# A hybrid attention and recurrence layer on one core: a fourth chunk of x turned by VectorE and DRAM, and the first stage written out by hand

## The chip, the cores and the metric

The kernel runs on one core of a Trainium2 chip. The metric is device time in microseconds (us); three runs of the kernel before gave a median of 626.83 us (626.64 to 627.36). Lower is better.

## The reference, cut to what matters

One layer takes x (512 tokens by 2048 features, float32), normalises it, projects it to 4608 columns, runs eight heads of attention and a gated linear recurrence on the parts, gates both, and projects back. The first step is the one that matters here:

```python
def rms_norm(x, w):
    xf = x.astype(jnp.float32)
    y = xf * lax.rsqrt(jnp.mean(xf * xf, axis=-1, keepdims=True) + EPS)
    return (y * w.astype(jnp.float32)).astype(x.dtype)

h = rms_norm(x, norm_w)
proj = jnp.einsum('bsd,de->bse', h, w_in)
q, k, v, g_attn, xr, g_lru = jnp.split(proj, SPLITS, axis=-1)
lru_out = lru_group(xr, ...)
mixed = jnp.concatenate([rms_norm(attn_out, attn_norm_w) * jax.nn.silu(g_attn),
                         rms_norm(lru_out, lru_norm_w) * jax.nn.silu(g_lru)], axis=-1)
return x + jnp.einsum('bse,ed->bsd', mixed, w_out)
```

## The kernel before

Every float32 operand of a product is split into a high part (rounded to float32r) and a low part (the rest), and each product is three TensorE passes: high by high, high by low, low by high (`mm3`, lines 152 to 155). ScalarE writes most high parts, VectorE the low parts.

The first stage is the projection to the first half of `xr` (`proj_feat(C_XR, a1, ...)`, lines 379 to 406 and 1212 to 1232). It needs x with features on the partitions, so that each of x's sixteen 128-feature columns has to be turned. x comes in eight chunks of 256 features (512 KB each, `xload`, tile `b`), and the matching rows of `w_in` in eight pieces of 512 KB (`wraw`, tile `wr`, a ring of three). A chunk c is 24 matmuls of 128x512: four output blocks, two columns, three passes. The mean square of x is not needed for this: its factor `rbc` multiplies the result at the end, so the squares (`xsquare`) can be late.

A chunk is turned in one of two ways. Chunks 0 to 4 (`TURNED = 5`): eight 128x128 transposes on TensorE against the identity (`xturn`, line 253), then ScalarE takes the high part out of PSUM (line 258) and VectorE the low one (line 261). Chunks 5 to 7: VectorE transposes 32x32 blocks within 32 partitions (`blocks`, line 281, tile `xu`), SyncE writes the result to DRAM (`put_aside`, line 289, `xd<-xu`, one transfer of 512 KB), and four transfers of 128 KB bring it back with the blocks on the right partitions (`bring_back`, line 296, `xu<-xd`, each to 32 partitions). Then ScalarE scales it in place (line 338) and rounds it (line 339), and VectorE subtracts (line 339). In this text, for a chunk n: Ln is its load, Wn the load of its weights, Bn its block transposes, Dn the write to DRAM, Rn the four reads back, Vn the scaling and splitting, Sn the splitting of Wn on ScalarE (line 218) and VectorE (line 219), Qn its four squares.

TensorE and SyncE run in written order through this stage. ScalarE and VectorE do so only up to step (1, 2) (`s2.close()`, line 1224); after that a scheduler orders them by priority and by `issue_after` links. What is issued when is set by a table of steps, `moves` (line 1195): a generator per chunk (`xchunk`) is advanced one phase at each mention. Each transfer on SyncE's queue waits until the eighth one before it has landed, as its eight completion semaphores go round.

The last projection to the output (`outputs`, lines 1008 to 1145) streams `w_out` in units; `feed2` (line 991) loads one unit's second row block, for the second half of the columns (g = 1) as one transfer of 512 KB (line 995).

Of the kernel before, what the change touches and what calls it, by code (L numbers as in the profile page):

```python
# [11 lines left out]
F32 = mybir.dt.float32  # L12
# [37 lines left out]


B = 32
TURNED = 5
NQ = P // B


# [7 lines left out]
def hybrid_kernel(  # L64
# [53 lines left out]
    def nm(s):  # L118
        cnt[0] += 1
        return f"{s}_{cnt[0]}"  # L120
# [108 lines left out]

    xh, xl = [None] * KT, [None] * KT  # L230
    ssq = const([P, NT, KT // 2], "ssq")
    highs, x_parts, squared = {}, [], []

    def xload(c, nk=1):

        xc = b4(shape=(P, NT, 2 * P))
        for k in range(nk):
            ks = slice(k * 2 * P // nk, (k + 1) * 2 * P // nk)
            cs = slice(c * 2 * P + ks.start, c * 2 * P + ks.stop)
            nc.sync.dma_start(xc[:, :, ks], xf[:, cs].rearrange("(t p) d -> p t d", p=P))  # L240
            yield xc

    def behind(those):
        stack = ExitStack()
        for ins in those:
            stack.enter_context(tc.issue_after(ins))
        return stack

    def xturn(xc, kk, then=None):
        pt = mm()  # L250
        for t in range(NT):
            ks = slice(kk % 2 * P, (kk % 2 + 1) * P)
            nc.tensor.transpose(pt[:, t * P : (t + 1) * P], xc[:, t, ks], ident)  # L253
        if then:
            then()
        xh[kk], xl[kk] = x2(), x2()
        with behind(split_done[-1] if kk > 3 else ()):
            highs[kk // 2] = nc.scalar.activation(
                xh[kk], pt, AF.Identity, scale=nw[:, kk : kk + 1]
            ).ins  # L260
        nc.vector.scalar_tensor_tensor(
            xl[kk], pt, nw[:, kk : kk + 1], f(xh[kk]), op0=ALU.mult, op1=ALU.subtract
        )

    def xsquare(xc, c):
        for t in range(NT):
            if c >= TURNED:
                nc.scalar.activation(
                    xc[:, t, :], xc[:, t, :], AF.Square, accum_out=ssq[:, t, c : c + 1]
                )  # L270
                continue
            square = nc.vector.scalar_tensor_tensor(
                xc[:, t, :], xc[:, t, :], 1.0, xc[:, t, :], op0=ALU.mult, op1=ALU.mult,
                accum_out=ssq[:, t, c : c + 1],
            )
            if c == 1:
                squared.append(square.ins)

    def blocks(u, t, src):

        nc.vector.transpose(
            u[:, :, :, t, :].rearrange("p b k r -> p k b r"),
            src.rearrange("p (k b c) -> p k b c", k=2, c=B),
        )
# [15 lines left out]
    def in_order(v):  # L300
        return v.rearrange("p (t i r) -> p i t r", t=NT, i=NQ)

    def xchunk(c):
        with tc.high_priority(AHEAD):
            (xc,) = xload(c)
        yield
        if c < TURNED:
            with tc.high_priority(AHEAD):
                for k in range(2):
                    xturn(xc, 2 * c + k)  # L310
            if c == 2:
                yield
            with behind(split_done[2][1:] if c == 2 else ()):
                xsquare(xc, c)
            yield
            return
        u, back = (
            ring.tile([P, NQ, 2, NT, B], F32, name=nm("xu")) for ring in (aring, hring)
        )
        with tc.high_priority(AHEAD), tc.issue_after(squared[-1] if c == TURNED else split_done[3][1]):  # L320
            for t in range(NT):
                blocks(u, t, xc[:, t, :])
        yield
        with tc.high_priority(AHEAD):
            there = put_aside(u, "xd", KT // 2 - TURNED)
        with tc.issue_after(highs[TURNED - 1]):
            xsquare(xc, c)
        yield
        with tc.high_priority(AHEAD):
            bring_back(back, there)  # L330
        yield
        with tc.high_priority(AHEAD), behind(split_done[-1]):
            for k in range(2):
                kk = 2 * c + k
                xh[kk], xl[kk] = x2(), x2()
                hi, lo = (in_order(v) for v in (xh[kk], xl[kk]))
                v = back[:, :, k]
                nc.scalar.activation(v, v, AF.Identity, scale=nw[:, kk : kk + 1])
                x_parts[:] = nc.scalar.copy(hi, v).ins, nc.vector.tensor_sub(lo, v, f(hi)).ins
        yield  # L340

    last_pool = [None]

# [8 lines left out]
    def rows(dst, col, dg):  # L352

        shape = [P, NT, P]
        part = [const([P, NT], nm("part")) for _ in range(2)]
        parts = [dg() for _ in part]
# [12 lines left out]
        yield  # L369
# [621 lines left out]
    def feed2(g, i, got):  # L991

        m = mixed[i][0] // (2 * P)
        x_ = in_wr()
        nc.sync.dma_start(x_.rearrange("p j e -> p (j e)"), block(m, 1, 2 * g, 2))
        if g == 0:
            z = in_av(1)
            nc.sync.dma_start(z[:, 0], t4[m])
        else:
            z = kept_t2.pop(i)  # L1000
            nc.vector.tensor_add(z, z, x_[:, 1:2])
        yield
        got.append(split(x_))
        yield
        got.append(split(z))
        yield
# [160 lines left out]
    with tc.high_priority():  # L1167
        xs, ws = xload(0, 2), wraw(w_in, 0, C_XR, 2)
        nc.scalar.dma_start(nw_st, norm_w.rearrange("(k p) -> k p", p=P))
        xc, raw = next(xs), next(ws)  # L1170
        next(xs), next(ws)
        table = const([P, 1], "table")
        nc.scalar.activation(table, ones[:, :1], AF.Exp)
        first = []

        def split_first():
            first.append(wsplit(raw, 0, nc.vector.tensor_copy))

        columns(nw, nw_st)
        xturn(xc, 0, split_first)  # L1180
        busy(WARM2)
    stats = xstats()
    chunks = [xchunk(c) for c in range(1, KT // 2)]

    raws = {}

    def fetch_x(c):
        with tc.high_priority(AHEAD):
            (raws[c],) = wraw(w_in, c * 2 * P, C_XR)

    def split_x(c):
        with tc.high_priority(AHEAD), behind(x_parts):
            given[c] = [wsplit(raws[c], k) for k in range(2)]

    moves = {
# [6 lines left out]
    }  # L1202

    def move(step):
        for name in moves.get(step, "").split():
            n = int(name[1])
            if name[0] == "x":
                next(chunks[n - 1])
            else:
                (fetch_x if name[0] == "w" else split_x)(n)  # L1210

    for step in proj_feat(C_XR, a1, first, given):
        if step is None:
            with tc.high_priority():
                first.append(wsplit(raw, 1, nc.vector.tensor_copy))
                xturn(xc, 1)
            xsquare(xc, 0)
            move(None)
            given[1] = wload(w_in, 2 * P, C_XR)
# [10 lines left out]
        if (c, e) in ((4, 3), (KT // 2 - 1, 0)):  # L1230
            with tc.high_priority(AHEAD), tc.issue_after(split_done[-1][1]):
                next(stats)

    s1.close()
    last_x = loads_done["lru"] = loads_done[nc.sync]
# [213 lines left out]
```

## Time and profile before

| | |
|---|---|
| median of three runs | 626.83 us |
| span of the profiled execution, first to last instruction | 625.3 us |
| median less that span | 1.5 us |
| TensorE busy | 620.3 us (99%) |
| VectorE busy | 494.8 us (79%) |
| ScalarE busy | 353.2 us (56%) |
| bytes moved by DMA | 127.61 MB |

The span is that of one execution under the profiler; the 1.5 us are what lies around it in the timed runs. TensorE's busy time is a union of modelled intervals: a matmul is shown as 0.39 us long while the next one starts 0.23 us after it, so the starts, not the durations, give its pace. For SyncE, a row of the timeline is the issue of a transfer, not the transfer.

### The profile page before, as it was taken

How to read it: one execution, taken by the hardware profiler on the slowest of the kernel's cores; microseconds unless marked ns; L12 is line 12 of the kernel's file. 1: busy time of each engine (PE TensorE's matmuls, PEld its weight loads, DVE VectorE, ACT ScalarE, POOL GpSimd, SP SyncE). 2: the span in 40 equal slices, each digit the busy share in tenths (PEclk: the TensorE clock that was granted, in tenths of full speed). 3: DMA queues.
4: the chain of work that ended last, by engine and by line, in shares of the span. 5: the costliest groups of instructions: out<-in, count | busy, mean ns of one | idle time of the engine just before them, and what ended most of it. 6: DMA issues, size and time to landing. Idle time of an engine off the chain costs nothing.

```text
span 625.3 us, 8281 instructions
## 1 busy us (share of the span) xinstructions
PE 620.3 (99%) x2758; PEld 512.8 (82%) x2758; DVE 494.8 (79%) x796; ACT 353.2 (56%) x617; POOL 101.7 (16%) x134
## 2 busy tenths in 40 slices
PE   9999999999999999999999999999999999999997
PEld 7888888888888888888888888888888888888886
DVE  5967979986699875987887888549979866886886
ACT  3764899479945823545485448428445633443441
POOL 0000210112003531622123223100310101010010
PEclk9999999999999999999999999999999999999999
DMA  8878785859774599479658646923995677896262
GB/s 289 293 210 253 179 206 163 175 136 197 236 231 140 169 235 250 103 204 273 186 175 258 201 140 192 265 79 106 261 248 185 210 253 240 293 327 233 68 202 101
DMA packets 73595, 127.61 MB, mean 204 GB/s; under 512 B 6617, under 2 KB 29265, under 8 KB 73553
## 3 DMA queue, kind: packets, MB, share of 16 engines
q1 hardware_dynamic: 65664, 109.65, 56.7%
q0 software_dynamic: 7712, 17.31, 14.3%
q8 instruction: 21, 0.34, 0.2%
q14 instruction: 22, 0.17, 0.1%
q10 hardware_dynamic: 176, 0.14, 0.1%
HBM read 110.29 MB, written 37.75 MB: 237 GB/s over the span
## 4 chain that ended last, share of the span: by engine, by line
PE 99%; DVE 0%; issue 0%; POOL 0%; POOLq 0%
PE pj L153 20%; PE pj L154 20%; PE pj L155 20%; PE mm L1029 14%; PE pj L1029 11%; PE mm L155 3%; PE mm L154 3%; PE mm L153 3%; PE pj L388 2%; PE mm L253 1%; PE mm L1156 1%; PE mm L829 0%; PE mm L367 0%; DVE cb L1058 0%; PE mm L189 0%
## 5 line engine op out<-in xcount | busy, mean ns | idle before, releaser
L153 PE MATMUL pj<-x,wh 128*128 128x512 f32 x368 | 143.5, 390 | 0.0
L155 PE MATMUL pj<-x,wl 128*128 128x512 f32 x368 | 143.2, 389 | 0.0
L154 PE MATMUL pj<-x,wh 128*128 128x512 f32 x368 | 143.2, 389 | 0.0
L218 ACT CAST wh<-wr 128x512 fp32r<-128x512 f32 x142 | 84.9, 620 | 78.9 <-PE pj L154 31.2
L219 DVE TENSOR_TENSOR wl<-wr,wh 128x512 fp32r<-128x512 f32 x144 | 99.9, 724 | 19.7 <-ACT wh L218 18.6
L881 ACT CAST wh<-wr 128x1024 fp32r<-128x1024 f32 (+1 forms) x72 | 60.8, 862 | 75.7 <-PE mm L1029 34.6
L882 DVE TENSOR_TENSOR wl<-wr,wh 128x1024 fp32r<-128x1024 f32 (+1 forms) x72 | 68.8, 985 | 30.5 <-ACT wh L881 30.3
L155 PEld LDWEIGHTS pj<-x,wl 128*128 128x128 f32 x368 | 69.1, 188 | 14.5
L153 PEld LDWEIGHTS pj<-x,wh 128*128 128x128 f32 x368 | 69.1, 188 | 14.3
L154 PEld LDWEIGHTS pj<-x,wh 128*128 128x128 f32 x368 | 69.1, 188 | 14.3
L153 PE MATMUL pj<-wh,x 128*128 128x512 f32 x192 | 74.7, 389 | 0.0
L155 PE MATMUL pj<-wh,x 128*128 128x512 f32 x192 | 74.7, 389 | 0.0
L154 PE MATMUL pj<-wl,x 128*128 128x512 f32 x192 | 74.7, 389 | 0.0
L905 POOL DMA_DIRECT2D t<-in_w_out_dram x40 | 33.5, 891 | 156.6 <-DMA t<-in_w_out_dram 99.4
L1029 PE MATMUL mm<-wh,ml 128*128 128x512 f32 x126 | 49.0, 389 | 0.0
L1029 PE MATMUL mm<-wh,mh 128*128 128x512 f32 x126 | 49.0, 389 | 0.0
L1029 PE MATMUL mm<-wl,mh 128*128 128x512 f32 x126 | 49.0, 389 | 0.0
L155 PEld LDWEIGHTS pj<-wh,x 128*128 128x128 f32 x192 | 36.0, 188 | 7.6
L153 PEld LDWEIGHTS pj<-wh,x 128*128 128x128 f32 x192 | 36.0, 188 | 7.5
L154 PEld LDWEIGHTS pj<-wl,x 128*128 128x128 f32 x192 | 36.0, 188 | 7.4
L706 POOL TENSOR_SCALAR p<-p,sm 128x512 f32<-128x512 f32 x32 | 24.3, 762 | 89.4 <-DVE sm L705 89.4
L1029 PE MATMUL pj<-wl,mh 128*128 128x512 f32 (+1 forms) x100 | 38.5, 385 | 0.0
(201 smaller groups left out, 1053.6 us busy)
## 6 DMA issues: line engine op xcount, KB each, us to landing
wr<-in_w_in_dram SPq DMA_DIRECT2D x71, 512.0 KB, 5.1
wr<-in_w_out_dram SPq DMA_DIRECT2D x24, 512.0 KB, 5.1
t<-in_w_out_dram POOLq DMA_DIRECT2D x40, 256.0 KB, 6.9
wr<-t SPq DMA_DIRECT2D x40, 256.0 KB, 5.4
pd<-u SPq DMA_DIRECT2D x16, 512.0 KB, 3.0
pt<-pd SPq DMA_DIRECT2D x64, 128.0 KB, 3.6
t<-in_w_out_dram SPq DMA_DIRECT2D x24, 256.0 KB, 5.4
t<-t SPq DMA_DIRECT2D x16, 256.0 KB, 5.1
```

The lines of the kernel that those rows point to most:

```text
L153: nc.tensor.matmul(acc, lh, rh, start=start, stop=False)
L154: nc.tensor.matmul(acc, lh, rl, start=False, stop=False)
L155: nc.tensor.matmul(acc, ll, rh, start=False, stop=stop)
L218: copy(hi, raw[:, k, :]).ins,
L219: nc.vector.tensor_sub(lo, raw[:, k, :], f(hi)).ins,
L253: nc.tensor.transpose(pt[:, t * P : (t + 1) * P], xc[:, t, ks], ident)
L388: nc.tensor.matmul(acc[e], w[:, e * P : (e + 1) * P], x_[2 * c + k], start=c == k == j == 0, stop=False,)
L706: last_pool[0] = nc.gpsimd.tensor_scalar(p, p, sm, 0.0, op0=ALU.mult, op1=ALU.add).ins
L881: nc.scalar.copy(hi[:, to], b)
L882: nc.vector.tensor_sub(lo[:, to], b, f(hi[:, to]))
L905: nc.gpsimd.dma_start(dst, src, accum_op=ALU.add)
L1029: nc.tensor.matmul(dst[s][:, es], lh[:, ts_], rh[:, es], start=i == ends_[0] and j == 0, stop=i == ends_[1] and j == 2,)
```

## The change

`TURNED` goes from 5 to 4: chunk 4 is no longer turned on TensorE but goes, as chunks 5 to 7 do, by VectorE and DRAM. The generator `xchunk` and its `issue_after` links are replaced by one short function per phase, and the table `moves` names every phase (L, W, T and H for turning, B, D, R, V, S, Q, and Z for the statistics). `s2.close()` moves from step (1, 2) to (5, 3), so that ScalarE and VectorE keep the written order until then. The squares come late: those of chunks 2 and 3 at step (2, 2), those of 6 and 7 at (3, 2). Apart from the first stage, `feed2` splits its load into two of 256 KB for g = 1 and the first six units.

```diff
-TURNED = 5
+TURNED = 4
...
+    def block_x(c):
+        units[c] = [ring.tile([P, NQ, 2, NT, B], F32, name=nm("xu")) for ring in (aring, hring)]
+        for t in range(NT):
+            blocks(units[c][0], t, chunk[c][:, t, :])
+
+    def aside_x(c):
+        units[c][0] = put_aside(units[c][0], "xd", KT // 2 - TURNED)
+
+    def back_x(c):
+        bring_back(units[c][1], units[c][0])
+
+    def whole_x(c):
+        for k in range(2):
+            v = units[c][1][:, :, k]
+            nc.scalar.activation(v, v, AF.Identity, scale=nw[:, 2 * c + k : 2 * c + k + 1])
+        for k in range(2):
...
+            nc.scalar.copy(hi, v)
+            nc.vector.tensor_sub(lo, v, f(hi))
...
-        x_ = in_wr()
-        nc.sync.dma_start(x_.rearrange("p j e -> p (j e)"), block(m, 1, 2 * g, 2))
+        if g and i < 6:
+            for j in range(2):
+                nc.sync.dma_start(x_[:, j], block(m, 1, 2 * g + j))
+        else:
+            nc.sync.dma_start(x_.rearrange("p j e -> p (j e)"), block(m, 1, 2 * g, 2))
...
-        (2, 0): "x5 x4 x5", (2, 1): "x4 w3", (2, 2): "x6 x7", (2, 3): "w4 s3",
+        (2, 0): "B6 D6 R5 W5 R6 Q5 Q5 V4",
...
-        if (c, e) == (1, 2):
+        if (c, e) == (5, 3):
             s2.close()
```

On SyncE, the queue from the twelfth transfer of the stage on. Before, `wr_60` is W3, `b4_61` and `b4_62` are L6 and L7, `wr_63`, `wr_69`, `wr_70` and `wr_85` are W4 to W7, the first `xd` is D5, the two together D6 and D7:

```order
L206 DMA wr_60_367<-in_w_in_dram 128x2x512
L240 DMA b4_61_375<-in_x_dram 128x4x256
L240 DMA b4_62_377<-in_x_dram 128x4x256
L206 DMA wr_63_385<-in_w_in_dram 128x2x512
L289 DMA xd_68_401<-xu_52_333 128x1024
L206 DMA wr_69_407<-in_w_in_dram 128x2x512
L296 DMA xu_53_334<-xd_68_401 32x4x256 x4
L206 DMA wr_70_413<-in_w_in_dram 128x2x512
L289 DMA xd_75_433<-xu_71_421 128x1024
L289 DMA xd_76_439<-xu_73_427 128x1024
L296 DMA xu_72_422<-xd_75_433 32x4x256 x4
L206 DMA wr_85_485<-in_w_in_dram 128x2x512
```

Now, from the same W3 (`wr_36`): `xd_39` is D4, `b4_40` L6, `wr_41` W4, `xu_38` R4, `b4_42` L7, then D5, D6, R5, W5 (`wr_69`), R6 and D7:

```order
L206 DMA wr_36_240<-in_w_in_dram 128x2x512
L288 DMA xd_39_248<-xu_37_242 128x1024
L239 DMA b4_40_250<-in_x_dram 128x4x256
L206 DMA wr_41_252<-in_w_in_dram 128x2x512
L295 DMA xu_38_243<-xd_39_248 32x4x256 x4
L239 DMA b4_42_258<-in_x_dram 128x4x256
L288 DMA xd_61_336<-xu_59_330 128x1024
L288 DMA xd_68_370<-xu_66_364 128x1024
L295 DMA xu_60_331<-xd_61_336 32x4x256 x4
L206 DMA wr_69_376<-in_w_in_dram 128x2x512
L295 DMA xu_67_365<-xd_68_370 32x4x256 x4
L288 DMA xd_80_422<-xu_78_416 128x1024
```

D4 and R4 now stand among the loads; D5 and R5 stand behind L7, where before D5 stood right behind W4, and W5 is behind R5 instead of ahead of it.

Further down the same queue, before, W7, R7, the small vectors, and W8 (`wr_134`, the first weights of the next stage):

```order
L206 DMA wr_85_485<-in_w_in_dram 128x2x512
L296 DMA xu_74_428<-xd_76_439 32x4x256 x4
L180 DMA vec_st_94<-in_conv_w_dram 32x128
L180 DMA vec_st_94<-in_conv_b_dram 8x128
L180 DMA vec_st_94<-in_lru_ba_dram 16x128
L180 DMA vec_st_94<-in_lru_bx_dram 16x128
L180 DMA vec_st_94<-in_lru_lambda_dram 16x128
L180 DMA vec_st_94<-in_attn_norm_w_dram 8x128
L180 DMA vec_st_94<-in_lru_norm_w_dram 8x128
L206 DMA wr_134_734<-in_w_in_dram 128x2x512
```

Now D7, W6, W8 (`wr_135`), R7, W7 and the first of the vectors:

```order
L288 DMA xd_80_422<-xu_78_416 128x1024
L206 DMA wr_81_424<-in_w_in_dram 128x2x512
L206 DMA wr_135_738<-in_w_in_dram 128x2x512
L295 DMA xu_79_417<-xd_80_422 32x4x256 x4
L206 DMA wr_82_430<-in_w_in_dram 128x2x512
L180 DMA vec_st_94<-in_conv_w_dram 32x128
```

W8 now stands ahead of R7 and W7, and since it takes the ring's place of W5, it waits until VectorE has split W5.

On ScalarE, from V5 (`xu_53`) to V6 (`xu_72`) before; `b4_62` is chunk 7, whose squares these are:

```order
L338 ACTIVATE xu_53_334<-xu_53_334,nw_95 128x4x128 x2
L339 CAST x2_81_465<-xu_53_334 128x4x4x32
L268 ACTIVATE b4_62_377,ssq_97<-b4_62_377 128x256
L339 CAST x2_83_470<-xu_53_334 128x4x4x32
L218 CAST wh_86_516<-wr_69_407 128x512
L218 CAST wh_88_520<-wr_69_407 128x512
L268 ACTIVATE b4_62_377,ssq_97<-b4_62_377 128x256 x3
L338 ACTIVATE xu_72_422<-xu_72_422,nw_95 128x4x128 x2
```

Now from V5 (`xu_60`) to V6 (`xu_67`); `b4_40` and `b4_42` are chunks 6 and 7:

```order
L335 ACTIVATE xu_60_331<-xu_60_331,nw_95 128x4x128 x2
L341 CAST x2_83_466<-xu_60_331 128x4x4x32
L341 CAST x2_85_470<-xu_60_331 128x4x4x32
L218 CAST wh_87_474<-wr_69_376 128x512
L218 CAST wh_89_478<-wr_69_376 128x512
L267 ACTIVATE b4_40_250,ssq_97<-b4_40_250 128x256 x4
L267 ACTIVATE b4_42_258,ssq_97<-b4_42_258 128x256 x4
L335 ACTIVATE xu_67_365<-xu_67_365,nw_95 128x4x128 x2
```

Eight squares now stand between S5 and V6, where three stood. On TensorE the eight transposes of chunk 4, which stood in the middle of chunk 2's matmuls, are gone; those of chunk 2 stand six matmuls later than before, together with those of chunk 3, and six matmuls of chunk 1 are left between them and chunk 2. From chunk 3 on, TensorE's order is the same in both.

More of the change, by code (lines that the diff above doesn't have):

```diff
@@ L256, in xturn @@
         xh[kk], xl[kk] = x2(), x2()
[L257 to L260, printed above, removed]
+        yield
+        nc.scalar.activation(xh[kk], pt, AF.Identity, scale=nw[:, kk : kk + 1])
+        yield
         nc.vector.scalar_tensor_tensor(
@@ L263, in xturn @@
         )
+        yield
     def xsquare(xc, c):
@@ L301, in in_order @@
         return v.rearrange("p (t i r) -> p i t r", t=NT, i=NQ)
[L303 to L340, printed above, removed]
@@ new lines, in hybrid_kernel, with load_x, turn_x, step_x @@
+    chunk, squares, halves, units = {}, {}, {}, {}
+    def load_x(c):
+        (chunk[c],) = xload(c)
+        squares[c] = xsquare(chunk[c], c)
+    def turn_x(c):
+        halves[c] = [xturn(chunk[c], 2 * c + k) for k in range(2)]
+        step_x(c)
+    def step_x(c):
+        for half in halves[c]:
+            next(half)
+    def square_x(c):
+        next(squares[c])
+    def block_x(c):
+        units[c] = [ring.tile([P, NQ, 2, NT, B], F32, name=nm("xu")) for ring in (aring, hring)]
+        for t in range(NT):
+            blocks(units[c][0], t, chunk[c][:, t, :])
@@ L1229, in hybrid_kernel @@
             columns(vec, vec_st)
-        if (c, e) in ((4, 3), (KT // 2 - 1, 0)):
-            with tc.high_priority(AHEAD), tc.issue_after(split_done[-1][1]):
-                next(stats)
+        if (c, e) == (KT // 2 - 1, 0):
+            next(stats)
     s1.close()
```

47 lines of the change are left out of this document (24 added, 23 removed), and 14 rows, old and new, of the table moves.

## The prediction

> **What bounds the kernel now.** I read the page first: its span, and the share of each engine in the chain of work that ended last.
>
> ```profile
> span 625.3 us, 8281 instructions
> ...
> PE 99%; DVE 0%; issue 0%; POOL 0%; POOLq 0%
> ```
>
> The chain is TensorE (PE) for its whole length. Then the waits, PE's own, up to 180 us:
>
> ```profile
> PE mm L1156 <- POOL ones L161: 1.1, 1, 1.1
> ```
>
> One wait, before the first instruction. So there is no stall to remove; the time falls only if PE gets less work, and rises by whatever PE is made to wait. Then PE's timeline in the first stage, where the change is:
>
> ```profile
> 5.70 1.30 PE L388 MATMUL pj<-x,wh 128*128 128x512 f32 x4
> ...
> 15.48 1.04 PE L253 MATMUL mm<-ident,b 128*128 128x128 f32 x8
> ...
> 19.92 0.47 PE L153 MATMUL pj<-x,wh 128*128 128x512 f32 x1
> ...
> 22.77 1.04 PE L253 MATMUL mm<-ident,b 128*128 128x128 f32 x8
> 23.57 0.47 PE L153 MATMUL pj<-x,wh 128*128 128x512 f32 x1
> 23.88 0.39 PE L154 MATMUL pj<-x,wh 128*128 128x512 f32 x1
> ...
> 26.41 0.39 PE L153 MATMUL pj<-x,wh 128*128 128x512 f32 x1
> ...
> 42.73 0.39 PE L153 MATMUL pj<-x,wh 128*128 128x512 f32 x1
> ```
>
> Chunk 2 starts at 19.92, chunk 3 at 26.41, chunk 6 at 42.73: three chunks of 24 matmuls in 16.32 us, 5.44 us each, 0.227 us per matmul. So chunk 4 starts at 31.85 and chunk 5 at 37.29. The row at 22.77 is chunk 4 being turned in the middle of chunk 2.
>
> **The gain.** Those eight transposes go. From 22.77 to 23.57 is 0.80 us, and the matmul behind them takes 0.31 us to the next start instead of 0.23: 0.88 us. From chunk 3 on everything in PE's order can start 0.88 us earlier: chunk 3 at 25.53, 4 at 30.97, 5 at 36.41, 6 at 41.85. This is all on the path, since PE is the path. A measurement of this kernel tells 0.2% (1.25 us) from no change; 0.88 us alone is less than that.
>
> **What the gain costs: the queue.** The price is a fourth round trip, 512 KB out and 512 KB back on SyncE's (SP) queue, in a stretch where that queue already carries x and the weights. The windows view, with DMA share and GB/s at the row's end:
>
> ```profile
> 20.00:24.00 4.00, 4.00 (x24) 3.40 (x23) 4.00 (x9) 2.13 (x4) 0.00 (x0) 1.00 1.04 390
> 24.00:27.00 3.00, 3.00 (x15) 2.45 (x14) 3.00 (x10) 2.78 (x10) 0.00 (x0) 1.00 0.37 131
> 34.50:41.50 7.00, 7.00 (x33) 5.79 (x32) 3.23 (x8) 3.47 (x7) 1.24 (x2) 1.00 0.93 223
> ```
>
> A plain transfer of 512 KB (524 kB) takes 524/390 = 1.35 us of a full queue. The stretch from 34.5 to 41.5 carries R6, W7 and R7 (223 GB/s for 7.0 us is 1561 kB, three transfers): (7.0 - 1.35)/2 = 2.8 us for a read back. It is twice as slow as a load, at the same busy share. The Trainium skill ("SBUF — State Buffer", section on the DMA port swizzle) has a reason: a transfer to 32 partitions reaches 8 of the 16 ports, about 218 GB/s at best, from which I estimate 2.4 us; the trace agrees in direction, and its 2.8 us is what I use. With 2.4 us the sum below would end 0.4 us lower.
>
> ScalarE's (ACT) and VectorE's (DVE) timelines give when things landed, and the times of their steps:
>
> ```profile
> 19.23 1.14 ACT L218 CAST wh<-wr 128x512 fp32r<-128x512 f32 x2 [0.82 <-DMA wr<-in_w_in_dram]
> ...
> 24.97 0.41 ACT L268 ACTIVATE b<-b 128x256 f32<-128x256 f32 x1
> ...
> 29.54 1.34 ACT L338 ACTIVATE xu<-xu,nw 128x512 f32<-128x512 f32 x2 [0.29 <-DMA xu<-xd]
> ...
> 38.10 1.34 ACT L338 ACTIVATE xu<-xu,nw 128x512 f32<-128x512 f32 x2 [3.53 <-DMA xu<-xd]
> 39.35 1.13 ACT L339 CAST x<-xu 128x512 fp32r<-128x512 f32 x2
> 40.38 1.14 ACT L218 CAST wh<-wr 128x512 fp32r<-128x512 f32 x2
> 42.98 1.34 ACT L338 ACTIVATE xu<-xu,nw 128x512 f32<-128x512 f32 x2 [1.45 <-DMA vec_st<-in_lru_lambda_dram]
> ```
>
> ```profile
> 13.66 0.41 DVE L272 SCALAR_TENSOR_TENSOR b<-b 128x256 f32<-128x256 f32 x1
> ...
> 16.33 1.43 DVE L281 STREAM_TRANSPOSE xu<-b 128x256 f32<-128x256 f32 x4 [1.21 <-DMA b<-in_x_dram]
> 17.68 1.37 DVE L261 SCALAR_TENSOR_TENSOR x<-mm,nw,x 128x512 fp32r<-128x512 f32 x2
> ...
> 39.99 1.29 DVE L339 TENSOR_TENSOR x<-xu,x 128x512 fp32r<-128x512 f32 x2 [2.17 <-ACT x L339]
> 41.20 1.29 DVE L219 TENSOR_TENSOR wl<-wr,wh 128x512 fp32r<-128x512 f32 x2
> ```
>
> And the issue of R5 on SP, with what SP waited for:
>
> ```profile
> 25.08 1.76 SPq L296 DMA_DIRECT2D xu<-xd  x4
> ```
>
> ```profile
> SPq L296 <- DMA xd<-xu: 9.4, 2, 5.0
> ```
>
> W3, the twelfth transfer, landed at 19.23 (ACT waited for it); the twelfth is W3 in both kernels and the sizes ahead of it are the same, so it lands at 19.2 again. D5 had landed when R5 was issued at 25.08, four transfers later: 5.85 us, against 4 x 1.35 = 5.4. So the queue serves in order, and a write is confirmed about 0.45 us late. R5, alone on the queue, was in at 29.54: 4.45 us from its first issue.
>
> Now the new order. D4 is ready when DVE has turned chunk 4's blocks: they take the place of chunk 1's squares at 13.66, plus 1.43 us, 15.1, long before its turn in the queue. Landings: W3 19.2, D4 19.2 + 1.35 + 0.45 = 21.0, L6 21.9, W4 23.25. R4 is issued when D4 has landed, at 21.0, and lands at 23.25 + 2.8 = 26.05. L7 stands behind R4, 27.4; D5 behind L7, 27.4 + 1.35 + 0.45 = 29.2 (before: 25.1); D6 30.1 and its confirmation 30.55. At 29.2 the queue is empty but for D6, R5 is issued and lands 4.45 us later, **33.65** (before: 29.5). Then W5 35.0, R6 37.8, D7 39.15 and 39.6, W6 40.5, W8 41.85, R7 44.65, W7 46.0. W8 waits for W5's split on DVE, at R5 + 4.4 = 38.05; R7 is queued behind that wait, but has to wait for D7 until 39.6 anyway, so that the wait costs nothing and W8's 1.35 us of queue are in the sum.
>
> **What the queue costs on PE.** From V6 at 38.10 the chain runs: first high part of W at about 41.0, first low part of W half way through the row at 41.20, 41.85, the second at 42.5. PE takes them at 0, 0.45 and 1.13 us into the chunk. The largest of 2.9, 3.75 - 0.45 and 4.4 - 1.13 is 3.3 us: V has to start 3.3 us ahead of its chunk.
>
> Chunk 4 (30.97): V4 by 27.7, R4 in at 26.05. In time by 1.6 us.
> Chunk 5 (36.41): V5 by 33.1, R5 in at 33.65. PE waits **0.55 us**.
> Chunk 6 (36.41 + 0.55 + 5.44 = 42.4): V6 by 39.1. R6 is in at 37.8, but ACT has V5 and S5 (38.10 to 41.52 in the rows: 3.42 us) and then eight squares at 0.40 us, 3.2 us, in front: 33.65 + 6.62 = 40.27. PE waits **1.17 us**.
> Chunk 7 (42.4 + 1.17 + 5.44 = 49.0): V7 by 45.7, R7 in at 44.65, ACT free at 43.7. In time.
>
> Sum: 0.55 + 1.17 - 0.88 = +0.84 us on the span of 625.3, and the same on the median, as the 1.5 us around the span are not touched: 626.83 + 0.84 = 627.67.
>
> **The other edits.** Chunks 2 and 3 are turned at (1, 2). Before, chunk 2 was turned at 15.48; now six matmuls later, 16.9 to 17.7, and chunk 3 to 18.5, with L3 in as the tenth transfer (at 16.33 before, where DVE waited for that one). ACT rounds chunk 2 by 18.8 and DVE subtracts by 19.6; PE wants the last of it at 20.8. 1.2 us of cover; beyond it each late 0.1 us is 0.1 us of PE. Chunk 3's low parts come behind B5 and W3's (1.43 and 1.29 us), 19.6 + 1.43 + 1.29 + 1.37 = 23.7, wanted at 25.8. The late squares cost nothing on DVE: it waits for ACT there (2.17 us at 39.99), and their sum is wanted only in chunk 7. On ACT they are the 1.17 us above. After the stage PE's order is unchanged, and its inputs move with it: nothing, as far as the covers seen hold. `feed2`: six loads become twelve halves. PE there:
>
> ```profile
> 500.00:600.00 100.00, 100.00 (x443) 82.74 (x442) 76.44 (x99) 41.38 (x55) 7.37 (x12) 1.00 0.69 229
> ```
>
> 443 matmuls in 100 us is the pace of 0.227 less a few missing records, and the DMA share is 0.69: six more issues are hidden. Bounds: nothing, or if the cover were gone a plain transfer's 1.35 us once. I take nothing.
>
> **The rivals.**
>
> *All in time.* PE never waits and the whole 0.88 us stays: 625.95. For it: the queue was almost idle from 24 to 27 us (0.37), so it had room for one more round trip. Against it: R5 would have to be in by 31.9 (chunk 6 at 41.85, less 3.3, less 6.62), 1.7 us earlier than the chain of landings gives.
>
> *The read backs are slower* (the other side). R6 was in at 38.10 and R7 at 42.98 with one load between: 4.88 - 1.35 = 3.5 us each, not 2.8. Then R4 lands at 26.75, D5 at 29.9, R5 at 34.35: chunk 5 waits 1.25 us, chunk 6 1.17 us; R6 39.2, R7 46.75, chunk 7 (49.7, so V7 by 46.4) 0.35 us. Sum 2.77 - 0.88 = +1.9 us, 628.7, slower. It decides where the waits exceed 2.13 us (1.25 + 0.88), that is from about 3.2 us a read back. For it: those two rows. Against it: R5 alone took 4.45 us with issue and confirmation.
>
> *Faster than the transposes.* From 5.70 to 19.92 PE does 48 matmuls and 28 transposes: 48 x 0.227 + 28 x 0.11 = 14.0 of 14.2 us. Even if the written order closed these 0.2 us too, the gain would be 1.1 us, 625.7. Faster by over 0.2% would take something that no row shows.
>
> **How the numbers follow.** Forecast, waits at chunks 5 and 6 with a net loss under 1.25 us: 0.39; its own range, from read backs of 2.4 and 3.2 us, 627.3 to 628.1. All in time: 0.20. Slower read backs: 0.37. What no row shows, faster: 0.04. So faster by over 0.2% has 0.04, within 0.2% 0.39 + 0.20 = 0.59, slower 0.37. The time is the forecast's, 627.7. The range starts at the all-in-time case, 625.9, and goes half a microsecond beyond the slower rival, 629.2, as the waits on ACT and the queue add up there; outside it stay the last case and what is still slower.
>
> **What would show it.** Right: PE's timeline has 32 transposes of x instead of 40, none inside chunk 2; starts of chunk 3 at about 25.5 and of chunk 4 at 31.0; PE waits named at chunk 5 (for the split of x or W, behind R5) and at chunk 6 (behind the squares); R5 issued near 29. Wrong: no PE wait before 60 us (the first rival), R5 issued well before 28, a wait at chunk 2 or 4, or a new wait near 500 to 600 us.

## The result, and the profile after

Five runs of the changed kernel gave a median of 630.95 us (630.49 to 632.16), five of the kernel before on the same chip 626.89 us (626.64 to 627.36): slower by 4.1 us, ratio 1.0063 (95% interval 1.0053 to 1.0074). The prediction was 627.7 us with a range up to 629.2. The profiled execution is the slowest of the five, 632.16 us, with a span of 630.0. What lies around the span is 2.1 to 2.2 us in each of the five runs; the kernel before has 1.5 us there in its profiled execution and 1.7 to 1.8 in its runs beside the experiments. So 0.3 to 0.6 us of the loss lie outside the span, where no profile names a wait. Medians below come from several chips; each ratio is taken against runs of the kernel before on the same chip.

The page's span and chain of waits:

```profile
span 630.0 us, 8303 instructions
...
PE 88%; DMA 5%; DVE 3%; ACT 2%; issue 1%; SPq 0%; POOL 0%; ACTq 0%; DVEq 0%; POOLq 0%
```

TensorE (PE) had 99% of this chain and has 88% now. The waits of PE say where (what waits, what it waits for, us in total, how often, the longest):

```profile
PE pj L153 <- ACT wh L218: 2.8, 2, 2.3
PE mm L1163 <- POOL ones L161: 1.1, 1, 1.1
PE mm L153 <- ACT b L529: 1.0, 1, 1.0
PE pj L155 <- DVE wl L219: 0.2, 1, 0.2
```

Only the second row stood in the profile before. PE's timeline around chunks 5 and 6:

```profile
36.61 0.39 PE L155 MATMUL pj<-x,wl 128*128 128x512 f32 x1
39.31 0.50 PE L153 MATMUL pj<-x,wh 128*128 128x512 f32 x1 [2.31 <-ACT wh L218]
39.64 0.40 PE L154 MATMUL pj<-x,wh 128*128 128x512 f32 x1
40.03 0.50 PE L155 MATMUL pj<-x,wl 128*128 128x512 f32 x1
40.37 0.40 PE L153 MATMUL pj<-x,wh 128*128 128x512 f32 x1
...
44.97 0.39 PE L155 MATMUL pj<-x,wl 128*128 128x512 f32 x1
45.82 0.50 PE L153 MATMUL pj<-x,wh 128*128 128x512 f32 x1 [0.46 <-ACT wh L218]
46.15 0.40 PE L154 MATMUL pj<-x,wh 128*128 128x512 f32 x1
46.71 0.50 PE L155 MATMUL pj<-x,wl 128*128 128x512 f32 x1 [0.16 <-DVE wl L219]
```

At a pace of 0.227 us per matmul the four steps from 36.61 to 40.37 should have taken 0.91 us and took 3.76: chunk 5 lost 2.85 us. Chunk 6 lost 1.16 in the same way. Two further losses are read off the same timeline: 1.28 us in stage two at 96 us, the third row of the waits, and 0.48 us more than before in the first four matmuls, whose row lasted 1.30 us before:

```profile
5.69 1.78 PE L391 MATMUL pj<-x,wh 128*128 128x512 f32 x4
```

These four start 0.59, 0.43 and 0.37 us after each other, before 0.45, 0.23 and 0.23; no wait is named there and the recorded clock is 1.00, so why they are slower is not shown. 2.85 + 1.16 + 0.48 + 1.28 - 0.88 = 4.9; the span grew by 4.7.

ScalarE's (ACT) and SyncE's (SP) timelines show what chunk 5 waited for. In ACT's rows L335 is V (scaling the read back), L218 S (splitting the weights); in SP's, L295 is a read back, L288 a write, L206 weights:

```profile
27.77 1.34 ACT L335 ACTIVATE xu<-xu,nw 128x512 f32<-128x512 f32 x2 [3.16 <-DMA xu<-xd]
...
35.26 1.34 ACT L335 ACTIVATE xu<-xu,nw 128x512 f32<-128x512 f32 x2 [4.08 <-DMA xu<-xd]
36.51 1.12 ACT L341 CAST x<-xu 128x512 fp32r<-128x512 f32 x2
38.63 1.14 ACT L218 CAST wh<-wr 128x512 fp32r<-128x512 f32 x2 [1.01 <-DMA wr<-in_w_in_dram]
...
42.89 1.32 ACT L335 ACTIVATE xu<-xu,nw 128x512 f32<-128x512 f32 x2
...
47.52 1.34 ACT L335 ACTIVATE xu<-xu,nw 128x512 f32<-128x512 f32 x2 [1.23 <-DMA xu<-xd]
```

```profile
22.85 2.77 SPq L288 DMA_DIRECT2D xd<-xu  x2
30.33 1.74 SPq L295 DMA_DIRECT2D xu<-xd  x4
32.17 0.40 SPq L206 DMA_DIRECT2D wr<-in_w_in_dram  x1
...
35.39 5.60 SPq L206 DMA_DIRECT2D wr<-in_w_in_dram  x2
```

R5 is issued at 30.33, when D5 has landed, and is in at 35.26; W5, issued at 32.17 behind R5, is in only at 38.63, and ACT stands for it for 1.01 us. Between V5 and V6 ACT does S5 and eight squares, up to 42.89. The windows view (us, then busy time of PE, PEld, DVE, ACT, POOL; the granted clock, the DMA share and GB/s end the row) shows the queue nearly idle (a DMA share of 0.25) while SP waits for D5, and then full at 250 GB/s:

```profile
29.50:32.00 2.50, 2.50 (x12) 2.06 (x12) 2.35 (x4) 1.68 (x4) 0.00 (x0) 1.00 0.25 75
32.00:39.00 7.00, 5.00 (x22) 3.77 (x21) 5.51 (x23) 2.73 (x5) 0.00 (x0) 1.00 1.01 250
```

### The profile page after: what moved, and what is told of

It reads as the page before. It is cut to its first block, busy times and chain, and to the rows that moved or that the text cites. A ratio compares the mean times of both kernels' runs of the same rounds, so it can differ in the third digit from the quotient of the medians.

```text
span 630.0 us, 8303 instructions
## 1 busy us (share of the span) xinstructions
PE 621.3 (99%) x2750; PEld 512.0 (81%) x2750; DVE 495.4 (79%) x792; ACT 354.6 (56%) x627; POOL 100.2 (16%) x134
## 4 chain that ended last, share of the span: by engine, by line
PE 88%; DMA 5%; DVE 3%; ACT 2%; issue 1%; SPq 0%; POOL 0%; ACTq 0%; DVEq 0%; POOLq 0%
PE pj L155 17%; PE pj L153 17%; PE pj L154 17%; PE mm L1036 14%; PE pj L1036 11%; PE mm L153 3%; PE mm L155 3%; PE mm L154 3%; DMA wr<-in_w_in_dram 2%; PE pj L391 2%; DMA xd<-xu 1%; DVE wl L219 1%; DVE k L512 1%; DMA k<-in_lru_wx_dram 1%; DMA k<-in_k_norm_w_dram 1%
## 5 line engine op out<-in xcount | busy, mean ns | idle before, releaser
L218 ACT CAST wh<-wr 128x512 fp32r<-128x512 f32 x142 | 84.3, 618 | 81.5 <-PE pj L154 29.1
```

What stands on the lines that cost most here:

```text
L218: copy(hi, raw[:, k, :]).ins,
```

## The experiments

Theory after this profile: the fourth round trip's transfers make R5 and W5 late. Rivals: the written order itself, the place of single transfers or of the squares, the split weights of the last projection, the work of the engines on chunk 4. Edits to `moves` are against the changed kernel; unchanged entries are left out. Each profile is of one execution.

**1. Chunk 4 on TensorE again, all else as changed.**

```diff
-TURNED = 4
+TURNED = 5
-(0, 2): "T1 H1 H1 L5 W3 B4 D4 L6 W4 R4 L7",
+(0, 2): "T1 H1 H1 L5 W3 L6 W4 L7",
-(2, 0): "B6 D6 R5 W5 R6 Q5 Q5 V4",
+(2, 0): "T4 H4 H4 B6 D6 R5 W5 R6 Q5 Q5",
-(1, 2): "T2 H2 H2 T3 H3 B5 D5 S3 H3 Q4 Q4",
-(2, 2): "S4 B7 D7 W6 R7 W7 Q2 Q2 Q3 Q3",
+(1, 2): "T2 H2 H2 T3 H3 B5 D5 S3 H3",
+(2, 2): "S4 B7 D7 W6 R7 W7 Q2 Q2 Q3 Q3 Q4 Q4",
```

> The changed kernel with chunk 4 turned on TensorE again, all else (written order to step 5, 3; late squares; halved loads in the last projection; W8 ahead of R7) left as it is. Theory A (the fourth round trip is the cost: it makes R5 and W5 late, and all later waits follow): the waits before chunks 5 and 6 and the one at 96 us go, TensorE has 0.9 us of transposes back, 626.9 to 627.3 us. Rival (the written order and the late squares cost it): the waits stay, 629.5 us or more.

Measured: 627.92 us (627.46 to 628.46, 11 runs), ratio 1.0010 (1.0001 to 1.0018). No wait is left at chunks 5 to 7 or at 96 us. The time is 0.6 us above the theory's range and far from the rival's. So most of the loss goes with moving chunk 4, which takes in both its transfers and the engines' work on it; run 12 parts the two. The written order, the late squares, the halved loads and W8's place together cost about 0.6 us.

**2. The halved loads alone, in the kernel before.**

```diff
+        if g and i < 6:
+            for j in range(2):
+                nc.sync.dma_start(x_[:, j], block(m, 1, 2 * g + j))
```

> The kernel before with one part of the change alone: the weights that stage two to six fetch two blocks at a time come as two transfers of one block. My reckoning: nothing, 626.9 to 627.5 us, within 0.2% of the kernel before. If two transfers in place of one cost the queue an issue that some later load waits for, a wait shows after 100 us and the time rises by 0.5 us or more.

Measured: 627.63 us (627.13 to 628.05, 11 runs), ratio 1.0003 (0.9994 to 1.0012). No effect that can be told from none.

**3. W5 ahead of R5.**

```diff
-(2, 0): "B6 D6 R5 W5 R6 Q5 Q5 V4",
+(2, 0): "B6 D6 W5 R5 R6 Q5 Q5 V4",
```

> The changed kernel with W5 issued ahead of R5, in the 4.7 us in which SyncE only waits for D5. Theory A: chunk 5 now waits for R5 alone, S5 starts when V5 ends (37.5 instead of 38.6), chunk 5's wait falls by 1.1 us and all behind it comes 1.1 us earlier: 629.9 us. Rival (order of the queue does not matter, R5 and W5 share the engines and end together whichever is first): R5 comes later by what W5 takes, 630.9 us or a little more.

Measured: 630.55 us (628.51 to 632.06, 6 runs), ratio 1.0047 (1.0032 to 1.0062). The profiled execution is the fastest one. There W5 fills the idle time in front of R5, R5 is in at 33.95 and PE's two waits for the split of the weights have shrunk:

```profile
PE pj L153 <- ACT wh L218: 0.3, 1, 0.3
PE pj L155 <- DVE wl L219: 0.3, 2, 0.2
```

Its other runs lie up to 3.5 us above it. The fastest run of the unedited kernel (run 14) has the same two rows of waits, so this profile does not show that W5's place made them shrink; the median is 0.6 us above what was expected of it, and W5's place is not what sets it.

**4. The squares of chunks 6 and 7 behind V6.**

```diff
-(3, 2): "V5 S5 Q6 Q6 Q7 Q7 Z0",
-(4, 2): "V6 S6 Z0",
-(5, 2): "V7 S7",
+(3, 2): "V5 S5",
+(4, 2): "V6 S6 Q6 Q6 Q7 Q7 Z0",
+(5, 2): "Z0 V7 S7",
```

> The changed kernel with the eight squares of chunks 6 and 7 behind S6 instead of ahead of V6. Theory A with waits that simply add up: chunk 6's 1.16 us go, 629.8 us. Theory A' (the end of the next stage is set by when its second piece of weights, W9, lands, since ScalarE is full there): chunk 6's wait goes, but the wait at 96 us grows by as much, from 1.3 to 2.4 us, and the time stays at 630.9 us.

Measured: 630.87 us (629.5 to 632.91, 6 runs), ratio 1.0058 (1.0042 to 1.0074). The wait at chunk 6 is gone, as expected, and the median is not lower. The wait at 96 us, which A' has growing, is not in this profile at all, so A' fails. What takes its place was new. PE stood for 2.0 us at chunk 5, and then:

```profile
36.50:38.40 1.90, 0.00 (x0) 0.00 (x0) 0.93 (x2) 0.75 (x3) 0.00 (x0) 1.00 1.08 336
38.50:39.25 0.75, 0.75 (x3) 0.32 (x3) 0.75 (x2) 0.42 (x1) 0.00 (x0) 1.00 1.04 404
39.25:42.75 3.50, 3.50 (x9) 2.73 (x10) 1.63 (x3) 3.03 (x6) 0.00 (x0) 0.51 0.71 219
42.75:44.00 1.25, 1.25 (x7) 1.04 (x6) 1.25 (x3) 1.25 (x6) 0.00 (x0) 1.00 1.08 279
```

From 39.25 to 42.75 PE's granted clock is 0.51 and a matmul takes 0.43 us instead of 0.227: some 1.7 us lost without any wait. Under a slower PE the next inputs have more time to come in. So this profile does not say by itself whether the moved squares or the slower PE ended the wait at chunk 6: in run 5, with the squares in their old place and the same slow stretch, it is gone too. Run 10 settles it.

**5. W8 held behind W7.** The load of the next projection's first weights stood ahead of R7 and waited there for W5's split (the SP row at 35.39).

```diff
+            with behind(hold.pop(c0, ())):
                 (raw,) = wraw(w, r0, c0)
...
+    hold[C_XR + SEQ] = (last_x,)
```

> The changed kernel with W8 behind W7 on SyncE. Theory A': SyncE no longer stands for 5 us at W8 waiting for the split of W5; R7, W7, the vectors and W9 are issued about 3 us earlier, the wait at 96 us (1.3 us) goes, chunks 5 and 6 wait as before: 629.7 us. Rival (the wait at 96 us is ScalarE's own order in the next stage): unchanged, 630.9 us.

Measured: 631.39 us (629.42 to 631.78, 5 runs), ratio 1.0054 (1.0041 to 1.0066). Chunk 5 waited 2.8 us, and the half clock followed again (x9 matmuls in 3.25 us, clock 0.50):

```profile
36.60:39.40 2.80, 0.04 (x1) 0.00 (x0) 1.29 (x2) 1.74 (x5) 0.00 (x0) 1.00 1.08 319
...
40.50:43.75 3.25, 3.25 (x9) 2.48 (x9) 0.44 (x2) 3.25 (x16) 0.19 (x1) 0.50 0.36 94
```

Three runs with a mean clock of 0.996 or 0.997 took 631.39 to 631.78 us, the two at 0.999 and 1.0 took 629.42 and 629.7. The wait at 96 us is gone, as expected, but run 4's profile has none either, with W8 in its old place. W8's place does not set the median.

**6. The same, with PE kept busy during the wait.**

```diff
+        if (c, e) == (4, 3):
+            again = mm()
+            for _ in range(22):
+                nc.tensor.matmul(again[:, : 2 * P], wv[:, :P], wv, start=True, stop=True)
```

> The variant with W8 held behind W7, and 22 small matmuls on ones (about 0.11 us each, 2.4 us) put between chunk 4's last matmul and chunk 5's first, where TensorE otherwise waits 2.85 us; what they compute is not used. If the half pace after that wait (granted clock 0.50 for 3.4 us, in three of five runs, at 631.4 to 631.8 us against 629.4 to 629.7 in the two others) comes from TensorE standing idle, no run shows it any more: clocks 0.999 to 1.0 and all runs near 629.5 us. If it comes from something else (load on the memory, chance), the share of runs at 0.997 stays and so does the median of 631.4 us.

Measured: 630.36 us (629.2 to 631.23, 5 runs), ratio 1.0045 (1.0032 to 1.0059), all five clocks 0.999 or 1.0. The same stretches, now with 23 matmuls in the first and the full pace in the second:

```profile
36.60:39.40 2.80, 2.64 (x23) 2.07 (x22) 1.29 (x2) 1.66 (x4) 0.00 (x0) 1.00 1.09 298
...
40.50:43.75 3.25, 3.25 (x15) 2.68 (x16) 0.60 (x2) 3.25 (x16) 0.12 (x1) 1.00 0.42 135
```

The half clock goes; the median is 1.0 us lower than run 5's on another chip, by the two ratios 0.6 us, with overlapping intervals, and not the 629.5 expected: with PE on time, the wait at chunk 6 is back (1.2 us over the pace in this profile).

**7. The changed kernel with the same small matmuls.**

```diff
+        if (c, e) == (4, 3):
+            again = mm()
...
```

> The changed kernel with 22 small matmuls on ones (0.11 us each, 2.4 us; what they compute is not used) between chunk 4's last matmul and chunk 5's first, where TensorE waits 2.84 us. If TensorE standing idle is what halves its clock for 3.4 us afterwards, none of the five runs shows a clock under 0.999, where three of five of the changed kernel stood at 0.996; the time falls only as far as no later wait takes up what the half clock cost, by 0 to 1 us, to 630 to 631 us. If the half clock comes from elsewhere, two or three of the five runs stand at 0.996 or 0.997 again.

Measured: 632.22 us (631.02 to 633.15, 5 runs), ratio 1.0074 (1.0060 to 1.0088); all five clocks 0.999 or 1.0. On the same chip the kernels of runs 8 and 9, without these matmuls, had the low clock in eight of nine runs; on run 6's chip those of runs 10 and 13 had it in four of ten. So the idle PE brings the half clock on. The time did not fall to the 630 to 631 us expected. Its profile has chunk 6 losing 1.2 us and a wait of 0.5 us at 96 us, which fits a later wait taking up what the half clock cost; since the changed kernel itself did not run on this chip, that is not shown.

**8. R6 behind D7 and W6.**

```diff
-(2, 0): "B6 D6 R5 W5 R6 Q5 Q5 V4",
-(2, 2): "S4 B7 D7 W6 R7 W7 Q2 Q2 Q3 Q3",
+(2, 0): "B6 D6 R5 W5 Q5 Q5 V4",
+(2, 2): "S4 B7 D7 W6 R6 R7 W7 Q2 Q2 Q3 Q3",
```

> The changed kernel with one move: R6's four transfers stand behind D7 and W6 in the queue, in place of right behind W5; W5 still follows R5. If a load shares the engines with the transfers queued behind it, W5 lands 2 us or more sooner than the 6.4 us after its issue that it took (38.6 us), ScalarE no longer waits for it before its split, and the chunk-5 wait of 2.84 us falls by about 1 us, to what R5's own lateness makes, 1.5 to 2.2 us; the run comes to 629 to 630 us if nothing else turns late. If the queue serves strictly in order, W5 still lands 6 us or more after its issue, behind R5, and the wait and the time stay as they were, 630.5 to 631.5 us.

W5's row of the DMA issues (KB, then us from issue to landing), in the changed kernel:

```profile
wr<-in_w_in_dram SPq DMA_DIRECT2D x1, 512.0 KB, 6.4
```

and with R6 moved:

```profile
wr<-in_w_in_dram SPq DMA_DIRECT2D x1, 512.0 KB, 5.0
```

W5 landed 1.4 us sooner after its issue although nothing ahead of it had changed, and PE's wait for ACT at chunk 5 fell from 2.3 to 1.5 us. By the expectation, strict order would have left it at 6 us or more. But in the eight profiles in which R6 follows W5 in this form (the changed kernel's and runs 1, 4, 5, 6, 7, 12 and 14) W5 took 5.2 to 6.9 us; 5.0 is under all of these, but by little. That W5 pays for R6 behind it is supported here, not shown. The time was 632.09 us (631.13 to 632.98, 5 runs), ratio 1.0074 (1.0062 to 1.0087), four of five with the low clock.

**9. The loads of x6 and x7 out of the way, with moves 3, 4 and 5.**

```diff
+(0, 2): "T1 H1 H1 L5 W3 B4 D4 W4 R4",
+(1, 2): "T2 H2 H2 T3 H3 B5 D5 L6 S3 H3 Q4 Q4",
+(2, 0): "W5 R5 B6 D6 L7 Q5 Q5 V4",
+(2, 2): "S4 W6 R6 B7 D7 R7 W7 Q2 Q2 Q3 Q3",
```

> The variant with all four moves, and the loads of x6 and x7 taken out of the way of the first read backs: L6 behind D5's write, L7 behind D6's, W5 ahead of R5 and W6 ahead of R6, the rest as it was; every transfer is still there. If the queue has room for four round trips as long as what is not yet needed stands behind what is, R4 lands about 2 us sooner, R5 starts about 2 us sooner (near 26.5 us in place of 28.5 to 30.3) and lands by 32 us, no matmul waits at chunks 5, 6 and 7, and the run comes to 626.3 to 627.5 us, with every clock at 0.999 to 1.0. If four round trips are more than the queue can carry beside the weights in this time, the lateness only moves on to chunk 6 or 7: a wait of 1 us or more there and 628.5 us or over.

Measured: 634.02 us (632.91 to 635.03, 4 runs), ratio 1.0107 (1.0092 to 1.0122). R5 was issued at 25.79, as expected, and in at 32.80, 0.8 us after the 32 expected, but VectorE's written order put x7's blocks and two chunks' squares ahead of V5's subtraction, and with L7 late PE waited 2.4 us for that. An earlier landing had been bought with another wait, and all four runs had the low clock.

**10. Moves 3, 4 and 5, and L7 behind D5.**

```diff
-(0, 2): "T1 H1 H1 L5 W3 B4 D4 L6 W4 R4 L7",
+(0, 2): "T1 H1 H1 L5 W3 B4 D4 L6 W4 R4",
-(1, 2): "T2 H2 H2 T3 H3 B5 D5 S3 H3 Q4 Q4",
+(1, 2): "T2 H2 H2 T3 H3 B5 D5 L7 S3 H3 Q4 Q4",
```

> The changed kernel with four edits to its tables: W5's load is issued ahead of R5, chunk 5's and 4's late squares stand behind V6 and S6 instead of ahead of V6, W8's load is held behind W7's, and L7's load stands behind D5's write instead of ahead of it, so that D5 lands about one load (1.35 us) sooner and R5 can be issued about that much sooner. If the 4 us are only the places of transfers and squares in the written order, the waits at chunk 5 (2.84 us), chunk 6 (1.16) and in stage two (1.28) go and the run comes to 625.9 to 627.5 us, level with the kernel before or up to 0.9 us under it. If the queue itself has no room for four round trips beside the weights, something stays late whatever the order: one of chunks 5, 6 and 7 waits 1 us or more and the run stays at 628.5 us or over.

Measured: 630.51 us (629.62 to 631.35, 5 runs), ratio 1.0049 (1.0036 to 1.0062). The squares that moved are those of chunks 6 and 7, as in run 4. The waits at chunk 6 and at 96 us are gone, this time in a profile with a clock of 1.0, and chunk 5 waits 1.9 us for ACT: R5 was issued at 28.49 and came in only at 35.71, behind D6 and W5.

**11. Every transfer by its due time, with moves 4 and 5.**

```diff
+(0, 2): "T1 H1 H1 L5 W3 B4 D4 W4 L6 R4",
+(1, 2): "T2 H2 H2 T3 H3 B5 D5 W5 S3 H3 B6 D6 Q4 Q4",
+(2, 0): "R5 L7 R6 Q5 Q5 V4",
+(2, 2): "S4 W6",
+(3, 2): "V5 S5 B7 D7 R7 W7 Q2 Q2 Q3 Q3",
```

> Four round trips once more, with every transfer placed by when its data is needed and no engine left behind a late one: D4 W4 L6 R4 D5 W5 D6 R5 L7 R6 W6 D7 R7 W7, W8 held behind W7, x6's blocks ahead of V4, x7's blocks and the squares of chunks 2 and 3 behind V5, those of chunks 4 to 7 behind V6 and S6. From 20.4 us to V7's due time at 44 us the queue has to move 13 transfers of 0.52 MB, 6.8 MB, which takes 290 GB/s; the windows of the variants so far gave 235 to 275 GB/s. If the order alone is at fault, all of it lands in time, no matmul of chunks 5 to 7 waits, and the time is 626.3 to 627.5 us. If the queue has no room, chunk 5, 6 or 7 still waits 1 us or more in some run, and the median is 628.5 us or over.

Measured: 629.96 us (629.24 to 630.36, 5 runs), ratio 1.0042 (1.0029 to 1.0054). In the profile, of the fastest run, the long wait at chunk 5 is gone; short ones stand at chunks 4, 6 and 7 instead (0.4, 1.0 and 0.9 us over the pace). No run has the low clock, but on this chip the unedited kernel (run 14) has none either. The time is that of the expectation's second half.

**12. The transfers of chunk 4 without their use.** Chunk 4 is turned on TensorE as in run 1, with B4, D4 and R4 back at their places; nothing reads what R4 brings.

```diff
-(0, 2): "T1 H1 H1 L5 W3 L6 W4 L7",
+(0, 2): "T1 H1 H1 L5 W3 B4 D4 L6 W4 R4 L7",
```

> The variant with chunk 4 turned on TensorE as before, and chunk 4's round trip put on the queue all the same: its blocks are turned on VectorE, written (D4) and read back (R4) at the changed kernel's places, into a buffer that nothing reads. TensorE has its 8 transposes back and no engine uses R4. If it is the load on the queue that makes x5 and W5 late, the chunk-5 wait of about 2 to 3 us comes back and the time rises from the 627.9 us of the variant without the transfers to 630.5 us or more. If the cost is in what the engines do with chunk 4 (the scaling, the copies and subtractions ahead of chunk 4's and 5's matmuls), the transfers run beside the work and the time stays at 627.5 to 628.5 us.

Measured: 629.38 us (628.24 to 630.33, 6 runs), ratio 1.0031 (1.0020 to 1.0043). It fell between the two expectations. By the two ratios the unused transfers cost 1.3 us over run 1. My expectation had left out that chunks 5 to 7 fall due 0.88 us later here, which hides that much of the lateness. In its one profile, 628.26 us, R5 is in at 33.62 where run 1 has 32.66; chunk 5 does not wait, and chunk 6 loses 1.2 us, which it does not in run 1. Three runs lie at 628.2 to 628.9 and three at 629.9 to 630.3.

**13. Read backs of 128 partitions.** Four transfers of 128 partitions and one block each; the kernel leaves out the exchange of blocks between partitions.

```diff
-        bring_back(units[c][1], units[c][0])
+        for b in range(NQ):
+            nc.sync.dma_start(
+                units[c][1][:, b].rearrange("p k t r -> p (k t r)"), units[c][0][:, b])
```

> The changed kernel, with the read back of each round trip as four transfers of 128 partitions and one block each in place of four transfers of 32 partitions and four blocks each; the blocks are then not exchanged between partitions, so x of chunks 4 to 7 stands in the wrong order, with the same bytes and the same number of transfers. If a read back takes 2.8 us because each of its transfers reaches only 32 partitions, it falls to about the 1.35 us of a load, R5 and W5 land 1.5 to 3 us sooner, the chunk-5 wait of 2.84 us falls under 1 us and the run to about 627.5 to 628.5 us. If the read backs go at the rate of all that the queue holds, their form costs nothing and the time stays within 0.7 us of the changed kernel's 630.95.

Measured: 629.83 us (629.6 to 631.36, 5 runs), ratio 1.0044 (1.0031 to 1.0057). R4 was in before 25.16 instead of 27.77, but R5 still took 4.5 us from issue and W5 6.1, and chunk 5 waited 1.9 us. So R4 comes in sooner in this form, but the form is not what makes chunk 5 late. The time lies between the two expectations. What lies around the span is 1.7 to 1.8 us here as in the kernel before, so 0.4 us of the lower time come from there.

**14. The changed kernel once more**, with no edit.

> The changed kernel once more, unchanged, beside the two others on one chip. Taken as the same kernel it gives 630.5 to 632.2 us, a chunk-5 wait of 2 to 3 us, and a clock of 0.996 or 0.997 in some of its five runs; a spread of 1.5 us or more between the runs belongs to it, where the kernel before spreads by under 1 us.

Measured: 630.04 us (628.9 to 631.45, 5 runs), ratio 1.0049 (1.0035 to 1.0063); all clocks 0.999 or 1.0, which I had not expected. Its profiled execution is its fastest, 628.9 us, and shows the same program with small waits:

```profile
PE mm L1163 <- POOL ones L161: 1.1, 1, 1.1
PE pj L155 <- DVE wl L219: 0.3, 2, 0.2
PE pj L153 <- ACT wh L218: 0.3, 1, 0.3
```

Its V and S rows on ACT:

```profile
34.07 1.34 ACT L335 ACTIVATE xu<-xu,nw 128x512 f32<-128x512 f32 x2 [4.06 <-DMA xu<-xd]
36.35 1.13 ACT L218 CAST wh<-wr 128x512 fp32r<-128x512 f32 x2
40.59 1.32 ACT L335 ACTIVATE xu<-xu,nw 128x512 f32<-128x512 f32 x2
```

## Why the prediction was wrong, step by step

**PE as the path, and the gain**: right. 32 transposes of x instead of 40; 0.88 us enter the sum above with their size.

**The landings**: the step that failed. "So the queue serves in order" took four transfers in a row from one place of the trace and made a timetable of eighteen landings from it. Loads with a read back behind them came in later than it says, by up to 3.6 us, and in the profiled execution the read backs came late too. Against it, in us:

| | predicted | profile, 632.16 us | second profile, 628.9 us |
|---|---|---|---|
| W4 in | 23.25 | 26.0 | 24.0 |
| R4 in, V4 starts | 26.05 | 27.77 | 26.60 |
| R5 issued (D5 landed) | 29.2 | 30.33 | 28.96 |
| R5 in, V5 starts | 33.65 | 35.26 | 34.07 |
| W5 in | 35.0 | 38.6 | 36.2 |
| V6 starts | 40.27 | 42.89 | 40.59 |

The times of W4 and W5 are issue and time to landing: W4 16.01 and 10.0, then 16.33 and 7.7; W5 32.17 and 6.4, then 30.80 and 5.4. In the second profile the timetable is right to 0.6 us except for W4 and W5; in the first everything comes 1 to 3.6 us later. Transfers that I took as served one after the other overlap. W5 was to land 1.35 us behind R5 and landed 3.4 and 2.1 us behind it. R6, behind W5, was in by 39.9 and 38.2 (its last transfer's issue and time to landing); counted on from R5 at 1.35 us for W5 and 2.8 for R6, the order gives 39.4 and 38.2. So the pair ends nearly where the order puts it, and the load in it comes 2.0 and 0.8 us late. What makes it more in one run than in another is open. The fourth round trip is not needed for it: in run 1 W5, issued at 29.06, took 6.2 us too; in the changed kernel it is issued 1.7 to 3.1 us later. A row of the kernel before had said so, with W7 between two read backs:

```profile
wr<-in_w_in_dram SPq DMA_DIRECT2D x1, 512.0 KB, 5.9
```

5.9 us from issue to landing, where one read back of 2.8 and one load of 1.35 in order make 4.15. I had used that stretch for the rate of a read back and not for the landing of the load. Nor was R5 of the kernel before "alone on the queue": SP issued W6 behind it at 26.94 and two writes from 27.43 on, before it was in at 29.54. The Trainium skill ("DMA: Bandwidth & Descriptors", section "Queues, rings and completion order") says that a transfer is split over up to 16 engines and that completion is not first in, first out per issuing engine. In the two profiles of the table W5 still came in behind R5, so they show the overlap and not a changed order.

**The wait at chunk 5**, 0.55 us predicted: 2.85 in the profile. V has to start 3.3 us ahead of its chunk, which was due at 36.84: R5 in at 35.26 makes 1.7 us, and S5's further wait for W5 1.0 us more. In the second profile chunk 5 loses 0.55 us, the predicted size, but partly by luck: PE itself came 0.6 us later to chunk 5 than the prediction has it, so R5 could be late by as much.

**The wait at chunk 6**, 1.17 us predicted: 1.16. In the second profile chunk 6 loses 1.0. The mechanism, eight squares between S5 and V6, is in ACT's rows, where V6 starts at 42.89 straight behind them, and in run 10, where the wait goes with the squares moved and PE at full clock. That the size came out although R5 was late is no luck: V6 follows V5 by 6.62 us of ACT's work and chunk 6 follows chunk 5 by 5.44, whenever R5 lands.

**"The wait costs nothing" (W8)**: not disproved. Holding W8 back (run 5) did not lower the median.

**"Its inputs move with it: nothing"**, for stage two: wrong in the profiled execution. ACT's second split of stage two's weights, in the kernel before and in the changed one:

```profile
54.41 1.15 ACT L218 CAST wh<-wr 128x512 fp32r<-128x512 f32 x2
```

```profile
59.42 1.14 ACT L218 CAST wh<-wr 128x512 fp32r<-128x512 f32 x2 [2.66 <-DMA wr<-in_w_in_dram]
```

It is 5.0 us late where PE's order is 3.6 us late (0.48 + 2.85 + 1.16 - 0.88), and 1.28 us were lost at 96 us; that the one led to the other is argued from the order of the work. In the second profile, which ran 3.2 us shorter, the same split starts at 55.24 and no wait stands at 96 us.

**Start and halved loads**: the loads cost nothing (run 2). For the start I named covers at chunks 2 and 3, which held; what was lost there, 0.48 us, was in the first four matmuls, for which the sum had no term. This loss differs from profile to profile: against the kernel before, the transposes behind those four start 0.1 us sooner in run 1, which has the changed kernel's order there, and 0.7 us later in run 14. The reading of the 443 matmuls was slightly off, as 100 us at 0.227 hold 441, so no record is missing; nothing hangs on it.

**"The same on the median, as the 1.5 us around the span are not touched"**: wrong by 0.3 to 0.6 us. Around the span lie 2.1 to 2.2 us in the changed kernel and in the runs that only reorder it, 1.9 us in runs 1 and 2, 1.7 to 1.8 us in runs 12 and 13. So neither the halved loads nor the number of transfers gives it alone, and what does is open.

**What no step had**: the half clock. It adds little where a later wait would have followed anyway, and so can make the repair of single waits look useless (runs 4 and 5).

**The rival "the read backs are slower"** was the nearest, with R5 at 34.35 and 628.7 us; it too kept the order of landings and stops short of the median.

So the fourth round trip causes most of the loss: without it 627.92, with its transfers unused 629.38, used 630.0 to 631.0. Free of what lies around it, the span's median grew over that of the kernel before on the same chip by 0.6 us in run 1, 2.0 in run 12 and 2.3 in run 14. Run 12 keeps VectorE's block transposes of chunk 4 too, and what the engines' further work on chunk 4 costs, against the 0.88 us that TensorE saves, is not parted. Six other orders of transfers and squares (runs 3, 4, 5, 8, 9, 10) and a full timetable (run 11) did not bring a median under 629.9. That no order could is not shown. Why the same program's read backs come in 1.2 us apart in two runs (R4 and R5 in the table) stays open.

## What to carry to other kernels

Before moving work from the engine that sets the time to the queue, take each kind of transfer's time from issue to landing in the place where it will stand, between the neighbours that it will have; here a timetable made from rates gave 627.7 us, while the kernel's fastest run took 628.9 and its medians were 630.0 and 630.95. 0.88 us of TensorE was bought with 1 MB more on a queue that feeds the next chunk, and TensorE then waited for that queue. When one wait is mended and the time stays, look at the granted clock and at the next chunk's wait before calling the mend useless.

## What was not expected of the hardware

After TensorE had stood for 1.5 to 2.8 us its granted clock could fall to half for about 3.4 us, beginning 0.8 to 1.8 us after it had started again: from 39.25 to 42.75 in run 4, after a stand of 2.0 us that ended at 38.45; from 40.5 to 43.9 in run 5, after 2.8 us that ended at 39.49; from 40.3 to 43.7 in run 8, after 1.5 us that ended at 38.47; from 39.7 to 43.1 in run 13, after 1.9 us that ended at 38.69. A stand of 2.31 us in the changed kernel's own profile and one of 1.9 us in run 10's were not followed by it, so the length of the stand alone does not decide. Small matmuls in the gap kept the clock at 0.999 or 1.0 in ten of ten runs. The Trainium skill ("TensorE: Matmul & The Clock Gate", section "HAM oscillation — how this bites in real kernels") gives the rule as no idle gaps over about 3.4 us; the length of the slow stretch agrees with the page's window, but here gaps of 1.5 to 2.8 us were enough, and the measurement decides.
